# A hybrid decoder layer on one core: another buffer for the bias table, a changed start and a changed end

## The chip, the core and the metric

The kernel runs on one core of one Trainium2 chip. The metric is the device time of one execution in microseconds (us), taken as the median over several runs. Beside the runs there is one execution recorded by the profiler; it has a span (first to last instruction of the program) and a device time of its own. The engines are named as the profile names them: PE is the matrix engine (PEld its weight loads), DVE the vector engine, ACT the scalar engine, POOL GpSimd, SP the engine that here only issues DMA transfers. A "q" behind an engine's name (SPq, ACTq) is its instruction queue, where DMA issues and semaphore instructions appear.

## The reference, cut to what matters

One layer, sequence 256, width 2048, everything in fp32:

```python
n = rmsnorm(h, g_mix);  q, k, v, u = split(n @ w_in)      # 2048 x 5120
a = attention(q, k, v) with a T5 bias: rel_bias[bucket(distance)] is added to the scores
c = silu(layernorm(depthwise_conv31(u_val * sigmoid(u_gate)) + conv_b))
h = h + concat(a, c) @ w_out                              # 2048 x 2048
h = h + cross_attention(rmsnorm(h), rmsnorm(mem))         # 4 heads
h = h + square(relu(rmsnorm(h) @ w1)) @ w2                # 2048 -> 8192 -> 2048
return rmsnorm(h, g_final)
```

With a sequence of 256 and blocks of 256 the block attention is plain causal attention within one block.

## The kernel before, in words

**Weights in 200 steps.** All weights are laid out as 200 pieces of 1 MB (128 x 2048 fp32), one per step. For step j, `raw[j]` is loaded (four buffers, so the load for step j+4 can only start when the split of step j is done with its buffer). ACT rounds it to fp32r into `wh[j]` (lines 157 to 160), DVE subtracts to get the rest `wl[j]`; for one step in seven between 8 and 47 (`on_pool`, line 162: steps 11, 18, 25, ...) POOL makes `wl[j]` in four quarters. Both have three buffers, so `wh[j]` can be written when PE is through with step j-3. PE then runs three products per pair of tiles (high x high, high x low, low x high; `mm3`, from line 101). A step is 48 products with 256 columns or 24 with 512.

**Order of the work.** The order on every engine is written out by hand: the loop over the 200 steps at line 916 issues, for step j, the hooks of the place "early", the load for step j+4, the split of step j+2, the hooks "pre" and "late", and then PE's products with the hooks "mid" and "post" in between and behind. Every engine carries out its own list in that order, so an instruction that waits holds up all behind it. The steps 0 to 15 are the convolution's inputs `u` in four blocks of four, 16 to 23 are v, 24 to 39 q and k, then mem's k and v, `w_out`, the cross attention, and from step 72 the MLP.

**Start.** SP issues all the first loads (lines 127 to 137): the gains, then in turn a quarter of the first group of x (`hT[0]`, line 130) and a quarter of the first weights (`raw[0]`, line 131), then the other groups of x with `raw[1]` to `raw[3]`. For steps 0 to 3 the splits are cut in quarters (line 334 for `wh`, line 186 for the activations `actH`). POOL builds the identity matrix and the ones (lines 139, 140).

**The bias table.** `make_bias` (line 260) takes an 8 x 512 tile from the `ring`, fills it on POOL with one row of bias values per head, and `spread_bias` (line 273, hook "early" of step 8) sends it with one DMA on ACT's queue to DRAM, 128 copies of each row (1024 pieces of 1532 bytes); `load_bias` reads it back in step 20 with each partition shifted by one. The `ring` (line 91) is a tag of seven 128 x 512 buffers, used by nearly all short-lived tiles: the gates of the convolution (`evac_u`, line 389, at steps 7, 8, 12 and 16), the squares of the statistics of mem (`st_m.group` at steps 8 to 11, ACT's line 210, added up by POOL on line 211). `evac_u(i)` also takes one of the four `hp` buffers, into which POOL writes zeros (line 391) and the gated values (line 396), and on which DVE then runs the 31 taps of the convolution as background work.

**End.** The last four steps (196 to 199) are the last column block of `w2`. Steps 196 and 197 do both halves of the rows; step 198 the rows 0 to 127 with the weights of 198 and 199, step 199 the rows 128 to 255 with the same weights. `finish(t, bank)` (line 835) adds the residual, squares with a sum, forms 1/sqrt with one Newton step, scales four 128 x 512 pieces and sends them out; `finish(0)` is issued ahead of the products of step 199, `finish(1)` behind them.

Of the kernel before, what the change touches and what calls it, by code (L numbers as in the profile page):

```python
# [9 lines left out]
F32 = mybir.dt.float32  # L10
# [5 lines left out]
P = 128  # L16
# [23 lines left out]
STEP_US = 5.25  # L40

# [36 lines left out]
def tile_hybrid_block(ctx: ExitStack, tc: tile.TileContext, xT, memT, w, par, rel, gfin, out):  # L78
# [50 lines left out]
    for i in range(4):  # L129
        nc.sync.dma_start(hT[0][:, i, :], xT[:, i, :])  # L130
        nc.sync.dma_start(raw[0][:, i * 512:(i + 1) * 512], w[0, :, i * 512:(i + 1) * 512])
# [6 lines left out]

    make_identity(nc, ident)
    pool.memset(ones, 1.0)  # L140
# [119 lines left out]
    def make_bias():  # L260
        rev = ring((8, 512))
        pool.memset(rev[:, 0:384], MASK)
        d = 0
        while d < T:
            e = d
            while e + 1 < T and bucket(e + 1) == bucket(d):
                e += 1
            b = bucket(d)
            pool.tensor_copy(rev[:, 255 - e:256 - d], relt[:, b:b + 1].to_broadcast([8, e - d + 1]))
            d = e + 1  # L270
        return rev
# [562 lines left out]

    def finish(t, bk):
# [6 lines left out]
        for i in range(2):  # L842
            c = slice(1536 + i * T, 1536 + (i + 1) * T)
            d = acc[t][:, c]
            dve.tensor_tensor(d, bk.ap[:, i * T:(i + 1) * T], d, op=OP.add)
            act.activation(ring()[:, 0:T], d, AF.Square, accum_out=ssq[:, 8 * t + 3 + i:8 * t + 4 + i])
            pool.tensor_mul(d, d, gb[3][:, i * T:(i + 1) * T])
            dve.scalar_tensor_tensor(part_ if i == 0 else v, ssq[:, 8 * t + 3 + i:8 * t + 4 + i], 1.0 / D, part_,
                                     op0=OP.mult, op1=OP.add)
# [3 lines left out]
        dve.tensor_scalar(a, a, -0.5, 1.5, op0=OP.mult, op1=OP.add)  # L853
        dve.tensor_tensor(r, y, a, op=OP.mult)
        for c in (0, 1, 2, 3):
            d = acc[t][:, c * 512:(c + 1) * 512]
            if c in (1, 3):
                act.activation(d, d, AF.Copy, scale=r)
            else:
                dve.tensor_scalar(d, d, r, None, op0=OP.mult)  # L860
            nc.sync.dma_start(out[rows, c * 512:(c + 1) * 512], d)

    for q in range(4):
# [4 lines left out]
        for cb in range(4):  # L868
            jc = j0 + 16 + 4 * cb
            if q == 3 and cb == 3:  # L870
                banks = []

                def first(kg, jc=jc):
# [10 lines left out]
                pe_units[jc + 3] = lambda jc=jc: (  # L884
                    act_stationary(jc + 2, banks, 2, s_pair, False, ts=(1,))
                    + act_stationary(jc + 3, banks, 3, s_pair, True, ts=(1,)))
# [145 lines left out]
```

## Time and profile before

| what | value |
|---|---|
| median of 3 runs | 1175.96 us (1175.51 to 1176.62) |
| the profiled execution, device time | 1174.24 us |
| its span | 1172.4 us |
| instructions | 18441 |
| DVE busy | 707.8 us (60%) |
| ACT busy | 540.9 us (46%) |
| POOL busy | 116.6 us (10%) |
| HBM read, written | 216.18 MB, 3.67 MB |

The profiled execution is 1.84 us longer than its span and 1.72 us shorter than the median of the runs. PE's clock is granted in two levels, full (2.4 GHz, shown as 1.00 or a 9 in the strip of slices) and half (1.2 GHz, 0.50). Matrix products overlap, so what counts is the distance between their starts and not their length. A wait is shown with the instruction that ended it.

### The profile page before, as it was taken

What the parts mean: (1) busy time and instruction counts of PE and PEld (TensorE: products, weight loads), DVE (VectorE), ACT (ScalarE), POOL (GpSimd) and SP (SyncE); (2) the same over time, 40 slices, a digit from 0 to 9 for tenths busy, and PEclk for the clock granted to TensorE, in tenths of its full rate; (3) what the DMA queues carried; (4) which work ended last, traced back from release to release, by engine and by line L of the source; (5) the groups of instructions that cost most, each with busy time, mean ns of one, the idle gap of its engine ahead of it and who ended that gap; (6) DMA issues with size and microseconds to landing.
All of it is one profiled execution on the core that took longest, in us unless ns stands there. A gap on an engine that the chain in (4) does not pass through costs nothing.

```text
span 1172.4 us, 18441 instructions
## 1 busy us (share of the span) xinstructions
PE 1149.8 (98%) x7976; PEld 1073.0 (92%) x7976; DVE 707.8 (60%) x821; ACT 540.9 (46%) x564; POOL 116.6 (10%) x100
## 2 busy tenths in 40 slices
PE   7989999999999999999999999999999999999996
PEld 7988899999999999999889999889999888999885
DVE  6669998787666668555444545454555454445443
ACT  7525444565666456554333444333444333444342
POOL 2453121012003003000000000000000000000112
PEclk9998999999999999999999999999999999999998
DMA  8865654444554535545655544655554655554632
GB/s 340 288 186 180 221 204 169 162 147 177 184 193 168 199 120 180 216 145 192 240 195 200 180 180 175 221 182 199 193 181 150 227 198 182 190 195 153 217 142 72
DMA packets 35000, 221.02 MB, mean 189 GB/s; under 512 B 3816, under 2 KB 6504, under 8 KB 9448
## 3 DMA queue, kind: packets, MB, share of 16 engines
q1 hardware_dynamic: 33888, 218.29, 52.0%
q10 hardware_dynamic: 1032, 1.57, 0.9%
q8 instruction: 62, 1.02, 0.3%
q14 instruction: 18, 0.15, 0.0%
HBM read 216.18 MB, written 3.67 MB: 188 GB/s over the span
## 4 chain that ended last, share of the span: by engine, by line
PE 93%; DMA 4%; ACT 1%; DVE 1%; issue 0%; SPq 0%; ACTq 0%
PE mm L101 87%; PE cv L101 3%; DMA dram_rev<-ring 3%; PE sm L101 2%; DMA raw<-in_w_dram 1%; DVE wl L67 1%; ACT wh L160 0%; PE sm L813 0%; PE sm L499 0%; PE sm L689 0%; DVE small L67 0%; ACT actH L186 0%; ACT L679 0%; ACT ring L679 0%; ACT ring L210 0%
## 5 line engine op out<-in xcount | busy, mean ns | idle before, releaser
L67 DVE TENSOR_TENSOR wl<-raw,wh 128x2048 fp32r<-128x2048 f32 (+1 forms) x205 | 447.1, 2187 | 305.5 <-ACT wh L160 301.1
L160 ACT ACTIVATE wh<-raw 128x2048 fp32r<-128x2048 f32 x195 | 373.5, 1915 | 505.0 <-PE mm L101 462.5
L101 PE MATMUL mm<-actH,wh 128*128 128x256 f32 x1600 | 452.4, 283 | 11.0 <-ACT wh L334 6.3
L101 PE MATMUL mm<-actH,wl 128*128 128x256 f32 x1600 | 449.0, 281 | 1.8 <-DVE wl L67 1.8
L101 PE MATMUL mm<-actL,wh 128*128 128x256 f32 x1600 | 448.4, 280 | 0.0
L101 PEld LDWEIGHTS mm<-actH,wh 128*128 128x128 f32 x1600 | 302.9, 189 | 11.7 <-ACT wh L334 6.5
L101 PEld LDWEIGHTS mm<-actH,wl 128*128 128x128 f32 x1600 | 303.1, 189 | 2.5 <-DVE wl L67 2.5
L101 PEld LDWEIGHTS mm<-actL,wh 128*128 128x128 f32 x1600 | 302.4, 189 | 0.3
L101 PE MATMUL mm<-wh,sH 128*128 128x512 f32 x512 | 199.3, 389 | 0.0
L101 PE MATMUL mm<-wh,sL 128*128 128x512 f32 x512 | 199.2, 389 | 0.0
L101 PE MATMUL mm<-wl,sH 128*128 128x512 f32 x512 | 199.2, 389 | 0.0
L101 PEld LDWEIGHTS mm<-wh,sL 128*128 128x128 f32 x512 | 96.1, 188 | 20.2
L101 PEld LDWEIGHTS mm<-wl,sH 128*128 128x128 f32 x512 | 96.1, 188 | 19.8
L101 PEld LDWEIGHTS mm<-wh,sH 128*128 128x128 f32 x512 | 96.1, 188 | 19.7
L67 DVE SCALAR_TENSOR_TENSOR cv<-hp,part,cv 128x256 f32<-128x256 f32 x240 | 97.7, 478 | 0.0
L897 POOL TENSOR_TENSOR acc<-acc,gb 128x512 f32<-128x512 f32 x6 | 12.1, 2041 | 669.8 <-ACT ring L833 669.8
L67 DVE TENSOR_TENSOR sL<-ring,sH 128x512 fp32r<-128x512 f32 x32 | 22.2, 692 | 67.1 <-ACT sH L801 67.1
L211 POOL TENSOR_TENSOR acc<-acc,ring 128x512 f32<-128x512 f32 x17 | 35.7, 2098 | 163.4 <-ACT ring L210 162.7
L170 POOL TENSOR_TENSOR wl<-raw,wh 128x512 fp32r<-128x512 f32 x24 | 32.4, 1383 | 98.0 <-ACT wh L160 98.0
L101 PE MATMUL mm<-wh,actH 128*128 128x512 f32 x96 | 38.2, 398 | 0.0
L101 PE MATMUL mm<-wh,actL 128*128 128x512 f32 x96 | 37.9, 395 | 0.0
L101 PE MATMUL mm<-wl,actH 128*128 128x512 f32 x96 | 37.9, 395 | 0.0
(156 smaller groups left out, 1039.1 us busy)
## 6 DMA issues: line engine op xcount, KB each, us to landing
raw<-in_w_dram SPq DMA_DIRECT2D x199, 1024.0 KB, 4.8
mem<-in_memT_dram SPq DMA_DIRECT2D x4, 512.0 KB, 8.0
out_dram<-acc SPq DMA_DIRECT2D x8, 256.0 KB, 3.1
hT<-in_xT_dram SPq DMA_DIRECT2D x3, 512.0 KB, 8.2
dram_rev<-ring ACTq DMA_DIRECT2D x1, 1532.0 KB
raw<-in_w_dram SPq DMA_DIRECT2D x4, 256.0 KB, 4.4
bias<-dram_rev SPq DMA_DIRECT2D x1, 1024.0 KB, 9.1
gb<-in_gfin_dram SPq DMA_DIRECT2D x4, 256.0 KB, 7.0
```

Source lines behind the costliest of these rows:

```text
L67: return op(out, *args, **kw)
L101: pe.matmul(o, lhsT=lhsT, rhs=rhs, start=not bk.begun, stop=stop, skip_group_check=True)
L160: act.activation(wh[j], raw[j], AF.Copy)
L170: pool.tensor_sub(wl[j][:, s], raw[j][:, s], wh[j].bitcast(F32)[:, s])
L211: eng.tensor_tensor(self.acc, self.acc, sq, op=OP.add)
L897: pool.tensor_mul(d, d, gb[cb])
```

## The change

- The tile of `make_bias` is taken from the four `hp` buffers, which the convolution's inputs use, and no longer from the `ring`.
- At the start the four quarters of `hT[0]` are issued from ACT's queue; the ones are written ahead of the identity; ACT runs a copy of one column, ahead of which its table is loaded, and PE transposes the ones 14 times into a bank that nobody reads.
- At the end step 199 does its columns in two halves, 256 columns each (48 products in place of 24). `finish` issues both adds, then both squares, then both small sums; the gains are multiplied by -0.5 beforehand on POOL (step 96), which saves one small operation; and the result goes out in five pieces, three scaled by DVE and sent by SP, two scaled and sent by ACT.

```diff
--- before.py
+++ after.py
@@ -38,6 +38,7 @@
 AHEAD = 2
 WOUT_ORDER = [(0, 0), (1, 0), (2, 0), (0, 1), (1, 1), (2, 1), (3, 0), (3, 1)]
 STEP_US = 5.25
+WARM = 14
 
 ROOM = 128
 ACT_SHIFT = {"H0": 16, "H1": 16, "H2": 112, "H3": 112, "L0": 16, "L1": 16, "L2": 112, "L3": 112}
@@ -127,7 +128,7 @@
     nc.sync.dma_start(part[:, 0:CB], par[:, 0:CB])
     load(0)
     for i in range(4):
-        nc.sync.dma_start(hT[0][:, i, :], xT[:, i, :])
+        act.dma_start(hT[0][:, i, :], xT[:, i, :])
         nc.sync.dma_start(raw[0][:, i * 512:(i + 1) * 512], w[0, :, i * 512:(i + 1) * 512])
     for g in range(1, 4):
         nc.sync.dma_start(hT[g], xT[:, 4 * g:4 * g + 4, :])
@@ -136,8 +137,13 @@
     relt = sb.tile([8, N_BUCKETS], F32, name="relt")
     nc.sync.dma_start(relt, rel)
 
+    pool.memset(ones, 1.0)
     make_identity(nc, ident)
-    pool.memset(ones, 1.0)
+
+    act.activation(rr[:, 14:15], ones[:, 0:1], AF.Copy)
+    warm = bank("sm")
+    for i in range(WARM):
+        pe.transpose(warm.ap[:, (i % 4) * P:(i % 4 + 1) * P], ones, ident)
 
 
     hooks = {}
@@ -258,7 +264,9 @@
     bias = sb.tile([P, 8, T], F32, tag="acc0", name="bias")
 
     def make_bias():
-        rev = ring((8, 512))
+
+        rev = sb.tile([P, 2, T + CONV_K - 1], F32, tag="hp", name="rev", bufs=4)
+        rev = rev.rearrange("p a b -> p (a b)")[0:8, 0:512]
         pool.memset(rev[:, 0:384], MASK)
         d = 0
         while d < T:
@@ -832,6 +840,12 @@
         d = acc[t][:, cb * 512:(cb + 1) * 512]
         act.activation(ring(), d, AF.Square, accum_out=ssq[:, 8 * t + cb:8 * t + cb + 1])
 
+    def prepare_gain():
+
+        for g in gb:
+            pool.tensor_scalar(g, g, -0.5, None, op0=OP.mult)
+    at("late", MLP0 + 24, prepare_gain)
+
     def finish(t, bk):
         st = small()
         part_, v, y, a = (st[:, i:i + 1] for i in range(4))
@@ -839,26 +853,42 @@
         rows = slice(t * P, (t + 1) * P)
         dve.tensor_reduce(v, ssq[:, 8 * t:8 * t + 3], axis=AX.X, op=OP.add)
         dve.tensor_scalar(part_, v, 1.0 / D, EPS, op0=OP.mult, op1=OP.add)
-        for i in range(2):
-            c = slice(1536 + i * T, 1536 + (i + 1) * T)
-            d = acc[t][:, c]
+        ends = [acc[t][:, 1536 + i * T:1536 + (i + 1) * T] for i in range(2)]
+        for i, d in enumerate(ends):
             dve.tensor_tensor(d, bk.ap[:, i * T:(i + 1) * T], d, op=OP.add)
+        for i, d in enumerate(ends):
             act.activation(ring()[:, 0:T], d, AF.Square, accum_out=ssq[:, 8 * t + 3 + i:8 * t + 4 + i])
             pool.tensor_mul(d, d, gb[3][:, i * T:(i + 1) * T])
+        for i in range(2):
             dve.scalar_tensor_tensor(part_ if i == 0 else v, ssq[:, 8 * t + 3 + i:8 * t + 4 + i], 1.0 / D, part_,
                                      op0=OP.mult, op1=OP.add)
         act.activation(y, v, AF.Sqrt)
         dve.reciprocal(y, y)
         dve.scalar_tensor_tensor(a, v, y, y, op0=OP.mult, op1=OP.mult)
-        dve.tensor_scalar(a, a, -0.5, 1.5, op0=OP.mult, op1=OP.add)
-        dve.tensor_tensor(r, y, a, op=OP.mult)
-        for c in (0, 1, 2, 3):
-            d = acc[t][:, c * 512:(c + 1) * 512]
-            if c in (1, 3):
+        dve.scalar_tensor_tensor(r, a, -3.0, y, op0=OP.add, op1=OP.mult)
+        for lo, hi, on_act in ((0, 256, False), (1280, 1664, True), (256, 768, False), (1664, 2048, True),
+                               (768, 1280, False)):
+            d = acc[t][:, lo:hi]
+            if on_act:
                 act.activation(d, d, AF.Copy, scale=r)
+                act.dma_start(out[rows, lo:hi], d)
             else:
                 dve.tensor_scalar(d, d, r, None, op0=OP.mult)
-            nc.sync.dma_start(out[rows, c * 512:(c + 1) * 512], d)
+                nc.sync.dma_start(out[rows, lo:hi], d)
+
+    def last_units(jc, banks):
+        units = []
+        for half in range(2):
+            o = banks[1].ap[:, half * T:(half + 1) * T]
+            for kg in (2, 3):
+                def unit(half=half, kg=kg, o=o):
+                    for i in range(4):
+                        hi, lo = s_pair(kg * 4 + i)
+                        c = slice(i * 512 + half * T, i * 512 + (half + 1) * T)
+                        mm3(banks[1], o, (hi[:, P:], lo[:, P:]), (wh[jc + kg][:, c], wl[jc + kg][:, c]),
+                            kg == 3 and i == 3)
+                units.append(unit)
+        return units
 
     for q in range(4):
         j0 = MLP0 + 32 * q
@@ -881,9 +911,7 @@
                 pe_units[jc + 2] = lambda jc=jc: (
                     act_stationary(jc + 2, banks, 2, s_pair, False, ts=(0,))
                     + act_stationary(jc + 3, banks, 3, s_pair, True, ts=(0,)))
-                pe_units[jc + 3] = lambda jc=jc: (
-                    act_stationary(jc + 2, banks, 2, s_pair, False, ts=(1,))
-                    + act_stationary(jc + 3, banks, 3, s_pair, True, ts=(1,)))
+                pe_units[jc + 3] = lambda jc=jc: last_units(jc, banks)
                 at("pre", jc + 3, lambda: finish(0, banks[0]))
                 at("post", jc + 3, lambda: finish(1, banks[1]))
                 continue
```

## Rows read from the trace of the kernel before

**Rows 1.** The page: engines, and the costliest groups (busy, mean ns | idle before).

```profile
PE 1149.8 (98%) x7976; PEld 1073.0 (92%) x7976; DVE 707.8 (60%) x821; ACT 540.9 (46%) x564; POOL 116.6 (10%) x100
...
L67 DVE TENSOR_TENSOR wl<-raw,wh 128x2048 fp32r<-128x2048 f32 (+1 forms) x205 | 447.1, 2187 | 305.5 <-ACT wh L160 301.1
L160 ACT ACTIVATE wh<-raw 128x2048 fp32r<-128x2048 f32 x195 | 373.5, 1915 | 505.0 <-PE mm L101 462.5
...
L897 POOL TENSOR_TENSOR acc<-acc,gb 128x512 f32<-128x512 f32 x6 | 12.1, 2041 | 669.8 <-ACT ring L833 669.8
```

**Rows 2.** The chain that ended last: start us, us, what.

```profile
50.25 36.14 DMA dram_rev<-ring
```

**Rows 3.** Timeline of ACT: start, duration (us), instruction [idle before <- what ended it].

```profile
86.41 0.63 ACT L210 ACTIVATE ring<-mem 128x512 f32<-128x512 f32 x1 [16.77 <-DMA dram_rev<-ring]
```

**Rows 4.** Timeline of PE around the gap.

```profile
83.84 0.28 PE L101 MATMUL mm<-actL,wh 128*128 128x256 f32 x1
83.96 0.28 PE L101 MATMUL mm<-actH,wl 128*128 128x256 f32 x1
88.89 0.58 PE L101 MATMUL mm<-actH,wh 128*128 128x256 f32 x1 [4.65 <-ACT wh L160]
...
91.21 0.58 PE L101 MATMUL mm<-actH,wl 128*128 128x256 f32 x1 [1.53 <-DVE wl L67]
...
97.34 0.28 PE L101 MATMUL mm<-actH,wh 128*128 128x256 f32 x1
```

**Rows 5.** A stretch: length, busy (count) PE PEld DVE ACT POOL, clock, DMA, GB/s.

```profile
91.00:97.00 6.00, 5.79 (x27) 5.79 (x28) 6.00 (x10) 3.31 (x4) 5.92 (x5) 0.50 0.50 176
```

**Rows 6.** The load of step 13: timeline of SP; DMA issues, us to landing.

```profile
58.14 0.33 SPq L125 DMA_DIRECT2D raw<-in_w_dram  x1
...
raw<-in_w_dram SPq DMA_DIRECT2D x1, 1024.0 KB, 18.7
```

**Rows 7.** Timeline of POOL, 55 to 73 us.

```profile
55.34 0.15 POOL L391 MEMSET hp<- 128x60 f32 x1
...
67.48 5.06 POOL L170 TENSOR_TENSOR wl<-raw,wh 128x512 fp32r<-128x512 f32 x4
```

**Rows 8.** Three stretches at the start, columns as in group 5.

```profile
3.00:4.00 1.00, 0.00 (x0) 0.00 (x0) 0.00 (x0) 0.60 (x1) 0.00 (x0) 1.00 0.64 172
...
6.00:10.00 4.00, 3.70 (x16) 3.48 (x17) 3.26 (x6) 2.81 (x6) 0.00 (x0) 1.00 0.97 318
10.00:14.00 4.00, 4.00 (x28) 4.00 (x28) 1.18 (x2) 1.14 (x2) 0.00 (x0) 1.00 1.01 419
```

**Rows 9.** Timeline of the first 16 us.

```profile
3.40 1.28 ACT L186 ACT_TABLE_LOAD   x1 [3.40 <-DMA hT<-in_xT_dram]
...
14.28 0.63 ACT L334 ACTIVATE wh<-raw 128x512 fp32r<-128x512 f32 x1 [1.95 <-DMA raw<-in_w_dram]
...
15.69 0.39 PE L101 MATMUL mm<-actH,wl 128*128 128x256 f32 x1 [0.22 <-DVE wl L67]
```

**Rows 10.** The end of the chain that ended last.

```profile
1162.85 0.43 DVE acc L67
...
1163.31 0.52 ACT ring L846 x2
...
1164.38 0.52 ACT ring L846 x2
...
1165.80 0.16 DVE small L67
...
1166.18 0.72 ACT acc L858
```

**Rows 11.** Timeline of the last products (PE) and last issues (SP).

```profile
1162.20 0.39 PE L101 MATMUL mm<-wl,sH 128*128 128x512 f32 x1
1162.42 0.39 PE L101 MATMUL mm<-wh,sL 128*128 128x512 f32 x1
...
1166.69 1.81 SPq L861 DMA_DIRECT2D out_dram<-acc  x4
```

## The prediction, made before the changed kernel was run

> **What bounds the kernel now.** I read the page first. PE is busy for 98% of the span while DVE is at 60% and ACT at 46% [rows 1], and ACT's main idle time before a split ended on PE: the weights are made ready in time and PE sets the pace. So time can only be won where PE is not at its pace, and I looked for such places along the chain that ended last. It runs through PE nearly everywhere, with three exceptions: the first 15.7 us, the last ten, and one piece of 36.14 us in between that is a single transfer, the bias rows on their way to DRAM [rows 2].
>
> **The gap.** The timeline of ACT says why that transfer is on the chain. The transfer reads a tile of the ring, and ACT's seventh new ring tile behind it (two gates of step 8, then the squares of mem: one in step 8, two in step 9, the second of two in step 10) gets the same buffer. ACT stands for 16.77 us until the transfer is done [rows 3]. Behind it in ACT's list is the split of step 13. PE, which has two steps of weights in hand, runs dry at 84.08, gets two products at 88.89 and is only under way again at 91.21, at half its clock [rows 4, 5]. The loss can be counted. Products start 0.12 us apart before the gap. The one at 97.34 is the 31st of step 13: two at 88.89, and 28 from 91.21 on, ahead of it. Without the gap the 31st would start at 84.08 + 30 x 0.12 = 87.7. So the gap costs 97.34 - 87.7 = 9.7 us, 2.7 of them because the 29 products from 91.21 on took 6.13 us where 3.5 would do.
>
> **Part 1, the source of the transfer.** It moves to an `hp` buffer, and the ring has no transfer in it any more. What comes next in place of the wait: ACT is free at 69.6 and takes the split of step 13 when its weights are there. They were issued at 58.14 and took 18.7 us [rows 6], so they are there at 76.8; this load does not depend on the gap. With 1.9 us on ACT and 2.2 on DVE [rows 1] the split ends at 81.0, or 82 with the squares of mem in front and POOL at work beside DVE. PE wants it at 84.08. That is 2 us to spare, the tightest place of my forecast, but to spare.
> The new wait is in `evac_u`. With four `hp` buffers given out in turn (the table, then u blocks 0, 1, 2) the block at step 16 gets the table's buffer back, and its zeros on POOL wait for the transfer, which ends at 50.25 + 36.14 = 86.4, perhaps some us later with more weights moving beside it. POOL has nothing behind these zeros but the gates of step 16 and the quarter splits of step 18; step 16 starts at 84.08 + 3 x 5.65 = 101 at PE's pace (48 products a step). About 14 us of cover. I put this part at 9.7 us; between 9.0 (small waits left) and 9.7.
>
> **Part 2, the start.** PE's pace begins at 15.69, and that is set by the landing of `raw[1]`: ACT begins its split at 14.28, after idling for it [rows 9]. The table load of 1.28 us in front of the first split, and the quarters of x, are not on that path by themselves. PE's first step is at half clock (16 products from 6.3 to 10 us) [rows 8]; it has 48 products and would end hardly before 14.6, so faster transfers alone would also win little. The change does both.
> DMA first: in the fourth us the engines were at a share of 0.64, and the us before and behind look alike; from 6 us on they are full [rows 8]. If a second queue fills these three us, the stream ends about 3 x 0.36 = 1.1 us earlier; if not, 0. A DMA issue takes 1.81 / 4 = 0.45 us on its queue [rows 11], and SP is rid of four. ACT has them now: 1.8 us from about 0.7, then the table load, so it is ready at about 4.2, ahead of the 4.7 of before. The idle share speaks for issuing as the limit, so I take 0.7, nearer to that row.
> The Trainium skill's page "Trainium Kernel Development and Optimization", section "Key Constraints", speaks against the second queue: transfers issued from several engines share the same 16 DMA engines, and only the issuing time is saved. By it alone the start would win 0 wherever the engines are full, and the sum below would be 10.5 in place of 11.2.
> The 14 transposes: no row has one at half clock. As bounds take 0 and the 0.23 us of a product with 256 columns at half clock (3.70 us by 16) [rows 8]: at most 14 x 0.23 = 3.2 us, from about 1.6 us, when POOL has the identity ready, to 4.8. PE had no work until 6.3, so they are free. They should let step 0 run at full clock, which is needed for the 0.7 but adds nothing to it.
>
> **Part 3, the end.** Step 199 has 48 products of 256 columns for 24 of 512. The long ones start 0.22 to 0.23 apart [rows 11], the short ones half of 0.24 [rows 4]: about 0.25 us more, on the path. What it could win is the first half's add and square beside the second half's products. I take that as not happening: no row shows DVE reading one half of a bank while PE writes the other; in the nearest row the add begins 0.43 us after the start of the bank's last product [rows 10, 11]. Bounds: nothing, or the 0.52 us of one square.
> The Trainium skill's page "PSUM — Partial Sum Buffer", section "PSUM bank collisions raise a hardware error", says that two engines in one bank and the same partitions collide even on different columns, so reads are to be held back by bank. By that rule the adds wait for all 48 products, as I have it.
> Even so the chain is shorter. The second square starts at once behind the first, at 1163.85 in place of 1164.38 [rows 10]: 0.53 us. One small operation of 0.16 plus its gap of 0.03 goes [rows 10]: 0.19. Together 0.72, less 0.25: 0.47.
> Output: the last issue of before ends 1166.69 + 1.81 - 1166.18 = 2.3 us after the scaling starts [rows 10, 11]. After, ACT scales 384 columns in about 0.57 (three quarters of its 0.72 plus a fixed part), issues in 0.45, and again: 2.0. So 0.3; between -0.2 (the megabyte itself is the limit) and 0.7. Sum of the end: 0.8, between 0 and 1.7.
> The four products of the gains on POOL in step 96 cost up to 2.0 us each [rows 1]; POOL idles for hundreds of us there, and DVE, which shares its time badly with POOL, is at 60%. They cost nothing; without that cover a few tenths.
>
> **Sum.** 9.7 + 0.7 + 0.8 = 11.2 us. The profiled execution had 1174.24; it would have 1163.0. The median of the runs is 1.72 above it, so 1175.96 - 11.2 = 1164.8 is what I predict.
>
> **The rivals.**
> *The front wins nothing* (the shared engines, part 2): 1175.96 - 10.5 = 1165.5. For: the share is 1.01 from 10 us on; against: 0.64 in the fourth. 10%.
> *The adds run beside the products*: 0.5 more, 1164.3. 6%.
> *The clock falls at the start*: step 0 done early, PE waits for `raw[1]`, and step 1 starts at half clock. The gap shows the price, 2.7 us: 1167.5. In the trace PE lost its clock over an idle time of 4.7 us [rows 4, 5]; here I expect 2 or less. 6%.
> *Step 13 late*: if its weights land 2 to 5 us later than 76.8, PE idles and may lose its clock: up to 1171. 5%.
> *The wait stays on the ring*, because its next tile in turn is also held by something slow: only parts 2 and 3 remain, 1174.5. Nothing in the trace shows such a holder. 2%.
> *Slower*: the block of step 8, not that of step 16, gets the table's `hp` buffer. Its zeros, done at 55.34 in the trace, then wait until 86.4 on POOL, and behind them are gates, three sums of squares and the quarters of step 11 [rows 7]. These began 12.1 us behind the zeros, so at 98.5; the first quarter is there at 99.8, and PE wanted it at 72.8. That is 27 us and 2.7 for the clock, less the 11.2: about 1194. It decides if a freed buffer is taken before those never used; the ring speaks against it, since there the freed buffer came round only as the seventh [rows 3]. 2%.
> The forecast itself keeps 69%.
>
> **The numbers.** Own range of the forecast 1163.2 to 1166.4. With both ends of the start and the end, the clock case and half a microsecond of spread between runs: 1162.5 to 1168.0. What is left out is the late split, the two cases of the wait and a part of the rest. 0.2% is 2.35 us, about what a measurement of this kernel can tell from no change; 0.96 for faster by more than that, 0.02 within, 0.02 slower.
>
> **What would show it.** In the profile of after: no wait of ACT for `dram_rev`; products 0.12 us apart through 84 to 97 us and a clock of 1.00 in that slice; DVE's split of step 13 ending 2 us ahead of PE; POOL's zeros of the fourth block behind the transfer, with PE undisturbed. At the start PE's pace from about 15.0. At the end both adds back to back behind the last product, the scaling about 2.6 us behind it, last issues from two queues. I would be wrong in the main term if PE still had a gap between 80 and 100 us, and in a small one if the first add of the last rows began before the last product.

## The result, and the profile after

In the first series of runs the changed kernel took 1163.05 us (median of 4 runs, 1162.63 to 1164.51), the kernel before 1176.29 (4 runs): a ratio of 0.9888, 95% interval 0.9871 to 0.9905, so 13.2 us less. In the last series it was 1162.9 (4 runs) against 1174.44 (9 runs): 0.9896 (0.9883 to 0.991), 11.5 us less. The prediction was 11.2 us less.

The first rows of the page of the changed kernel, to hold against [rows 1]:

```profile
span 1162.7 us, 18533 instructions
...
PE 1148.5 (99%) x8014; PEld 1072.3 (92%) x8014; DVE 709.2 (61%) x821; ACT 540.3 (46%) x565; POOL 123.0 (11%) x104
```

The span is 9.8 us shorter; DVE, ACT and PE have the same work. The helper lines have moved by a few (L101 is now L102, L160 is L166).

**The gap.** The list of waits from 60 to 105 us (who waited for what: us in total, times, longest):

```profile
ACT wh L166 <- DMA raw<-in_w_dram: 8.0, 1, 8.0
...
POOL hp L399 <- DMA dram_rev<-rev: 1.2, 1, 1.2
PEld sm L102 <- DVE acc L68: 1.1, 1, 1.1
```

ACT's wait for the bias transfer [rows 3] is not there. In its place ACT waits 8.0 us for the weights of step 13, which costs PE nothing at step 13 itself, and POOL 1.2 us for the transfer before it clears the buffer of the fourth block, long before that block's step. The load of step 13, as in [rows 6]:

```profile
57.40 0.33 SPq L126 DMA_DIRECT2D raw<-in_w_dram  x1
...
raw<-in_w_dram SPq DMA_DIRECT2D x1, 1024.0 KB, 20.0
```

It landed at 57.40 + 20.0 = 77.4. The timeline of PE, where [rows 4] had the gap:

```profile
83.21 0.28 PE L102 MATMUL mm<-actH,wl 128*128 128x256 f32 x1
83.33 0.28 PE L102 MATMUL mm<-actH,wh 128*128 128x256 f32 x1
83.44 0.28 PE L102 MATMUL mm<-actL,wh 128*128 128x256 f32 x1
...
91.69 0.28 PE L102 MATMUL mm<-actH,wl 128*128 128x256 f32 x1
92.88 0.61 PE L102 MATMUL sm<-ones,acc 128*128 128x1 f32 x4 [0.92 <-DVE acc L68]
93.35 0.36 PE L102 MATMUL mm<-actH,wh 128*128 128x256 f32 x1
```

The product at 83.33 is the first of step 13, with 0.12 us to its neighbours on either side: no gap. The five us in which PE stood are now full, at full clock (stretch, with the columns of [rows 5]):

```profile
84.00:89.00 5.00, 5.00 (x45) 5.00 (x44) 5.00 (x8) 1.99 (x2) 3.81 (x5) 1.00 0.65 229
91.00:97.00 6.00, 5.08 (x44) 4.88 (x43) 6.00 (x9) 1.31 (x2) 0.00 (x0) 1.00 0.54 194
```

But between 91.69 and 92.88, within step 14, PE stands for one small product, the column sums of mem's statistics, which needs a sum from DVE. Two rows of DVE's timeline say why:

```profile
90.22 2.28 DVE L68 TENSOR_TENSOR wl<-raw,wh 128x2048 fp32r<-128x2048 f32 x1
92.42 0.41 DVE L68 TENSOR_TENSOR acc<-acc 128x256 f32<-128x256 f32 x1
```

The sum (0.41 us, from 92.42) is queued behind the split of step 15, and that split behind all that the late weights of step 13 have pushed back. The profiles below bear this out: PE stands here where that load took 19.9 us or more, and not where it took 18.9 or less.

**The start.** The same instructions as in [rows 9], and the transposes:

```profile
1.49 3.25 PE L146 MATMUL sm<-ident,ones 128*128 128x128 f32 x14 [1.49 <-POOL ident masks.py:199]
2.62 1.28 ACT L143 ACT_TABLE_LOAD   x1 [2.62 <-issue]
...
13.53 0.63 ACT L342 ACTIVATE wh<-raw 128x512 fp32r<-128x512 f32 x1 [1.95 <-DMA raw<-in_w_dram]
...
14.94 0.38 PE L102 MATMUL mm<-actH,wl 128*128 128x256 f32 x1 [0.22 <-DVE wl L68]
```

```profile
3.00:4.00 1.00, 1.00 (x7) 1.00 (x6) 0.00 (x0) 0.99 (x2) 0.00 (x0) 1.00 0.91 171
...
6.00:10.00 4.00, 2.84 (x17) 2.24 (x18) 2.23 (x5) 2.17 (x5) 0.00 (x0) 1.00 1.04 374
```

The DMA share of the fourth us rose from 0.64 to 0.91 [rows 8]. From 6 to 10 us PE did 17 products in 2.84 us of busy time in this profile, where it had needed 3.70 for 16. Its pace starts at 14.94, 0.75 us earlier.

**The end.** The last product, the end of the chain that ended last, POOL's part, and the last issues, as in [rows 10, 11]:

```profile
1153.98 0.28 PE L102 MATMUL mm<-wh,sL 128*128 128x256 f32 x1
...
1154.30 0.44 DVE acc L68
...
1154.76 0.92 ACT ring L860 x4
...
1155.70 0.40 DVE small L68
...
1156.80 0.17 DVE rr L68
...
1157.06 0.62 ACT acc L873
...
1155.34 1.41 POOL L861 TENSOR_TENSOR acc<-acc,gb 128x256 f32<-128x256 f32 x2 [4.24 <-ACT ring L860]
...
1157.38 1.31 SPq L877 DMA_DIRECT2D out_dram<-acc  x3
...
1158.76 0.34 ACTq L874 DMA_DIRECT2D out_dram<-acc  x1
```

Both adds begin behind the last product (1153.98 + 0.28 = 1154.26). The scaling starts 2.70 us after the first of them on DVE (1157.00; on ACT 1157.06), where it was 3.33 [rows 10]; from there to the end of the span it is 5.68 us in place of 6.26.

The ledger of the two profiled executions, each line a difference of two times in the same rows of both:

| part | before | after | won, us |
|---|---|---|---|
| PE's pace starts | 15.69 | 14.94 | 0.75 |
| from there to the first product of step 14 | 83.78 | 74.04 | 9.74 |
| step 14 | 6.23 | 7.28 | -1.05 |
| first product of step 15 to that of step 199 | 1051.51 | 1052.09 | -0.58 |
| step 199, to the end of its last product | 5.60 | 5.91 | -0.31 |
| last product to the scaling | 3.37 | 2.74 | 0.63 |
| scaling to the end of the span | 6.26 | 5.68 | 0.58 |
| span | 1172.44 | 1162.68 | 9.76 |

In the other profiles with the same end 2.74 repeats within 0.01 us and 5.68 within 0.03, but for one 5.57. The kernel before was profiled once.

### The profile page after: what moved, and what is told of

It is laid out like the page before. It is cut to its first block, busy times and chain, and to the rows that moved or that the text cites. A ratio compares the mean times of both kernels' runs of the same rounds, so it can differ in the third digit from the quotient of the medians.

```text
span 1162.7 us, 18533 instructions
## 1 busy us (share of the span) xinstructions
PE 1148.5 (99%) x8014; PEld 1072.3 (92%) x8014; DVE 709.2 (61%) x821; ACT 540.3 (46%) x565; POOL 123.0 (11%) x104
## 4 chain that ended last, share of the span: by engine, by line
PE 93%; DMA 3%; DVE 2%; ACT 1%; issue 0%; ACTq 0%; POOL 0%; DVEq 0%
PE mm L102 87%; PE cv L102 3%; DMA raw<-in_w_dram 2%; PE sm L102 2%; DVE wl L68 1%; ACT wh L166 0%; DVE cv L68 0%; DMA hT<-in_xT_dram 0%; PE sm L821 0%; PE sm L507 0%; PE sm L697 0%; DVE small L68 0%; ACT actH L192 0%; POOL hp L404 0%; ACT L687 0%
## 5 line engine op out<-in xcount | busy, mean ns | idle before, releaser
L166 ACT ACTIVATE wh<-raw 128x2048 fp32r<-128x2048 f32 x195 | 373.6, 1916 | 512.2 <-PE mm L102 463.7
L102 PE MATMUL mm<-actH,wh 128*128 128x256 f32 x1600 | 449.9, 281 | 2.5 <-ACT wh L342 2.5
L102 PE MATMUL mm<-actH,wl 128*128 128x256 f32 x1600 | 446.4, 279 | 0.7 <-DVE wl L68 0.7
L102 PE MATMUL mm<-actL,wh 128*128 128x256 f32 x1600 | 446.0, 279 | 0.0
L102 PEld LDWEIGHTS mm<-actH,wh 128*128 128x128 f32 x1600 | 300.3, 188 | 3.5 <-ACT wh L342 3.3
L102 PEld LDWEIGHTS mm<-actH,wl 128*128 128x128 f32 x1600 | 300.6, 188 | 1.3 <-DVE wl L68 1.3
L102 PEld LDWEIGHTS mm<-actL,wh 128*128 128x128 f32 x1600 | 299.7, 187 | 0.3
L102 PE MATMUL mm<-wh,sH 128*128 128x512 f32 (+1 forms) x520 | 200.7, 386 | 0.0
L102 PE MATMUL mm<-wh,sL 128*128 128x512 f32 (+1 forms) x520 | 200.6, 386 | 0.0
L102 PE MATMUL mm<-wl,sH 128*128 128x512 f32 (+1 forms) x520 | 200.6, 386 | 0.0
L102 PEld LDWEIGHTS mm<-wh,sH 128*128 128x128 f32 x520 | 97.7, 188 | 19.7
L102 PEld LDWEIGHTS mm<-wh,sL 128*128 128x128 f32 x520 | 97.7, 188 | 19.7
L102 PEld LDWEIGHTS mm<-wl,sH 128*128 128x128 f32 x520 | 97.7, 188 | 19.5
L102 PE MATMUL mm<-wh,actH 128*128 128x512 f32 x96 | 38.2, 398 | 0.0
L102 PE MATMUL mm<-wh,actL 128*128 128x512 f32 x96 | 38.0, 395 | 0.0
L102 PE MATMUL mm<-wl,actH 128*128 128x512 f32 x96 | 38.0, 395 | 0.0
```

What stands on the lines that cost most here:

```text
L102: pe.matmul(o, lhsT=lhsT, rhs=rhs, start=not bk.begun, stop=stop, skip_group_check=True)
L166: act.activation(wh[j], raw[j], AF.Copy)
```

## The experiments

The theory: the gap is worth 9.7 us and is gone, what its transfer does to the load of step 13 gives about 1 us of it back, the start and the end bring a little under 1 us each. The rivals: the start, the end or the clock bring more than that, or the convolution's buffers are held up.

### The table back on the ring

```diff
-        rev = sb.tile([P, 2, T + CONV_K - 1], F32, tag="hp", name="rev", bufs=4)
-        rev = rev.rearrange("p a b -> p (a b)")[0:8, 0:512]
+        rev = ring((8, 512))
```

> The changed kernel with the bias table back on the ring; start and end as changed. Theory (the wait on the ring is worth 9.7 us, less 1.1 given back at the sums of mem): ACT waits 15 us or more for the transfer again, PE has one gap of about 5 us near 83 us and some 29 products at half clock behind it, and the time is 1174 us, about 2 below the kernel before. Rival (start and end bring more than the one profile shows, since the medians lie 13.2 us apart and the two spans only 9.8): 1172.5 or less.

Measured: 1172.59 us (10 runs) against 1175.09 (13 runs), ratio 0.998 (0.997 to 0.9989). Waits from 60 to 105 us, and the two stretches around the gap (columns as in [rows 5]):

```profile
ACT ring L216 <- DMA dram_rev<-ring: 15.6, 1, 15.6
...
DVE wl L68 <- ACT wh L166: 10.3, 1, 10.3
...
82.00:88.00 6.00, 1.85 (x14) 1.44 (x12) 1.18 (x1) 3.64 (x5) 1.81 (x2) 0.99 0.14 52
88.00:95.00 7.00, 5.83 (x28) 5.83 (x29) 7.00 (x10) 4.27 (x4) 6.92 (x5) 0.52 0.41 151
```

The wait, the gap and the half clock (28 products from 88 to 95 us at 0.52) are back, with the start and the end of the changed kernel in place. The gap cost 8.3 us in this profile (82.36 us from the start of PE's pace, 14.81, to the first product of step 14, 97.17, where the changed kernel needs 74.04), 9.7 in the profile of before. The time lies between the two figures expected: 2.5 us below the kernel before, with an interval from 1.3 to 3.5, which holds the theory's 2; the rival's bound of 1172.5 was missed by 0.1 us only. By medians, each against the kernel before in its own series, 9.0 to 10.7 us of the changed kernel's gain (11.5 and 13.2, less 2.5) hang on the buffer alone. The rest is for start and end together, and for the gap, which came out shorter here.

### A buffer of its own for the table

```diff
-        rev = sb.tile([P, 2, T + CONV_K - 1], F32, tag="hp", name="rev", bufs=4)
-        rev = rev.rearrange("p a b -> p (a b)")[0:8, 0:512]
+        rev = sb.tile([8, 512], F32, name="rev")
```

> The changed kernel with a buffer of its own for the bias table, neither the ring's nor the convolution's. Theory (POOL's new wait for the transfer is covered): no wait of POOL for the transfer, and the span within 0.5 us of the changed kernel's. Rival (the convolution's buffers are held up by it): 1 us or more below it.

Measured: span 1160.3 us, one run of 1162.09, and POOL's wait for the transfer gone. That is 2.4 us below the first profile of the changed kernel, but only 1.2 below its second (next experiment), and the first product of step 14 comes 74.03 us after the start of PE's pace, to the hundredth as in the changed kernel. What differs is step 14 (6.10 us against 7.28 and 6.22), and the long stretch behind it. The span missed the theory's 0.5 us and met the rival's figure. But five later versions that leave the table in the convolution's buffer have the same 6.10 in step 14 (the start of before, no transposes, one queue, the bank of its own and the long products), and 1051.1 to 1051.6 us from step 15 to 198 as this one has 1051.12. So the convolution's buffer holds nothing up; the span alone would not have told.

### The changed kernel again

> The changed kernel once more, for a second profile. Theory: PE's pace starts at 14.9 us, no gap at 84 us, a gap of about 1.1 us near 92 us, last product to end about 8.4 us; the spread between runs is in the small gap and in the transfers, so each part repeats within 0.5 us. Rival (one of the parts itself varies by 2 us or more between runs, which would explain why the medians differ by more than the profiles): the start of PE's pace or the gap near 92 us differs by more than 1 us.

Measured: span 1161.5, and in the last series another profile with 1161.25. The three profiles of the same program, with two more:

| profile | pace starts | to step 14 | step 14 | steps 15 to 198 | span |
|---|---|---|---|---|---|
| changed, first | 14.94 | 74.04 | 7.28 | 1052.09 | 1162.7 |
| changed, second | 14.70 | 74.04 | 6.22 | 1052.21 | 1161.5 |
| changed, third | 14.41 | 74.03 | 7.27 | 1051.21 | 1161.2 |
| own buffer | 14.71 | 74.03 | 6.10 | 1051.12 | 1160.3 |
| before | 15.69 | 83.78 | 6.23 | 1051.51 | 1172.4 |

The wait in step 14 was there in two of three profiles. The weights of step 13 landed 20.0, 18.9 and 19.9 us after their issue in the three, and 17.7 to 18.5 us after it in the six versions with 6.10 in step 14 (own buffer and the five named there), so the wait hangs on about one us of this load. The stretch that PE paces alone, steps 15 to 198, differs by 1 us between runs of one program, and the -0.58 of the ledger is such a difference. The theory's "each part within 0.5 us" was too tight by that, and the rival's threshold for step 14 was just passed.

### The sums of mem one step later

```diff
-    at("mid", 14, st_m.totals, 2)
-    at("mid", 14, lambda: st_m.chain(r_m), 2)
+    at("mid", 15, st_m.totals, 2)
+    at("mid", 15, lambda: st_m.chain(r_m), 2)
```

> The changed kernel with the column sums of mem's statistics one step later (step 15). Theory (in the changed kernel PE stands 1.1 us in step 14 for a small DVE sum queued behind the late split of step 15): that gap is gone, span 1.1 us below the changed kernel's. Rival (the delay only moves to the next thing that DVE owes PE): a gap of 0.5 us or more shows up at the split of step 15 or 16, span less than 0.5 us below.

Measured: span 1160.8, step 14 at 5.66 us (48 products and nothing else), step 15 at 6.09 with the sums in it, and no product of PE waits for DVE from 60 to 105 us. But this run did not put the theory to the test: its load of step 13 took 18.5 us, as in the versions without the wait, whose steps 14 and 15 take the same 11.75 us together (6.10 and 5.65). That the edit removes the wait where the load is late is argued from the first profile alone: the sum ends there at 92.8, and the middle of step 15 would come at about 97.4 (an estimate: step 15 from 94.6, and the sums 2.8 us behind its start, as in step 14).

### The start of before

```diff
-        act.dma_start(hT[0][:, i, :], xT[:, i, :])
+        nc.sync.dma_start(hT[0][:, i, :], xT[:, i, :])
...
+    make_identity(nc, ident)
     pool.memset(ones, 1.0)
-    make_identity(nc, ident)
-
-    act.activation(rr[:, 14:15], ones[:, 0:1], AF.Copy)
-    warm = bank("sm")
-    for i in range(WARM):
-        pe.transpose(warm.ap[:, (i % 4) * P:(i % 4 + 1) * P], ones, ident)
```

> The changed kernel with the start of before: all transfers on SP, no transposes of the ones, no early table load. Theory (the start is worth 0.7 to 1.0 us, through the landing of the second weights): the second weights are split from 14.2 us on, PE's pace starts at 15.7 us, and everything behind is about 0.8 us later than in the changed kernel. Rival (the start brings nothing that lasts, as the same 16 DMA engines carry all): PE's pace starts within 0.3 us of the changed kernel's 14.9.

Measured: the second weights split from 13.73, PE's pace from 15.14. Between the two theories: 0.2 later than the changed kernel's first profile and 0.7 later than its third. One profile does not decide it.

### Without the transposes

```diff
-    warm = bank("sm")
-    for i in range(WARM):
-        pe.transpose(warm.ap[:, (i % 4) * P:(i % 4 + 1) * P], ones, ident)
```

> The changed kernel without the 14 transposes. Theory (step 0 then runs at half clock to about 11 us, but waits for its quarters and for the second weights at 13.5 us anyway): PE's pace starts within 0.4 us of the changed kernel's 14.9. Rival (the clock is what the start wins): 0.7 us later or more.

Measured: PE's pace from 14.19, earlier than in any run with the transposes. They win nothing here. Without them the products of step 0 start 0.21 us apart up to 9.7 us and 0.12 later; the first product of step 1 still follows at 13.60, and what sets the pace is the low part of the second weights, for which PE waits 0.19 us even then.

The other profiles say the same. With the transposes, step 0 starts with products 0.12 us apart in four profiles of eleven; in the other seven, the changed kernel's third among them, they are 0.21 apart from the fourth on, as without. The pace does not follow it: with two queues it starts at 14.68 in the mean of the four and in that of the other six alike.

### One queue again, transposes and table load kept

```diff
-        act.dma_start(hT[0][:, i, :], xT[:, i, :])
+        nc.sync.dma_start(hT[0][:, i, :], xT[:, i, :])
```

> The changed kernel with the four quarters of x back on SP's queue, transposes and early table load kept. Theory (the idle share of the DMA engines before 5 us is what the second queue fills): the split of the second weights starts about 14.2 us in place of 13.5, PE's pace 0.7 us later. Rival (shared engines, the second queue brings nothing): both within 0.2 us of the changed kernel.

Measured: PE's pace from 16.18. The split of the second weights in the three runs (one queue; start of before; no transposes), with the fourth us of the first and the last, and the stretch from 6 to 10 us of the first:

```profile
14.78 0.63 ACT L342 ACTIVATE wh<-raw 128x512 fp32r<-128x512 f32 x1 [1.95 <-DMA raw<-in_w_dram]
...
3.00:4.00 1.00, 1.00 (x7) 1.00 (x6) 0.00 (x0) 0.49 (x1) 0.00 (x0) 1.00 0.54 139
6.00:10.00 4.00, 3.92 (x17) 3.70 (x18) 2.70 (x5) 2.60 (x6) 0.00 (x0) 1.00 1.00 291
```

```profile
13.73 0.63 ACT L338 ACTIVATE wh<-raw 128x512 fp32r<-128x512 f32 x1 [2.10 <-DMA raw<-in_w_dram]
```

```profile
12.78 0.63 ACT L339 ACTIVATE wh<-raw 128x512 fp32r<-128x512 f32 x1 [2.10 <-DMA raw<-in_w_dram]
...
3.00:4.00 1.00, 0.00 (x0) 0.00 (x0) 0.00 (x0) 0.99 (x2) 0.00 (x0) 1.00 0.63 163
```

The share of the fourth us is 0.54 with one queue and 0.91 in the changed kernel, but it does not sort the runs: without the transposes it is 0.63 with two queues, and the kernel before had 0.64 with one. What sorts them is what had been moved by 10 us: 2.07 to 2.09 MB in the three profiles with one queue, 2.41 to 2.55 MB in the eleven with two. Most of that difference arises from 6 to 10 us, where the share is near 1 either way (291 to 318 GB/s with one queue, 358 and more with two). All profiles of the study together: with one queue PE's pace starts at 15.14, 15.69 and 16.18 (mean 15.67), with two queues at 14.19 to 15.04 in eleven profiles (mean 14.64). The groups don't overlap, though the nearest two are 0.1 us apart. By the means the second queue is worth 1.0 us; single runs scatter by half a us around it. The early table load was not tried by itself.

### The last half columns in a bank of their own

```diff
+        if t == 1:
+            dve.tensor_tensor(ends[1], tail[0].ap[:, T:2 * T], ends[1], op=OP.add)
...
+        tail.append(bank("mm"))
...
-            o = banks[1].ap[:, half * T:(half + 1) * T]
+            bk = (banks[1], tail[0])[half]
+            o = bk.ap[:, half * T:(half + 1) * T]
...
-                        mm3(banks[1], o, (hi[:, P:], lo[:, P:]), (wh[jc + kg][:, c], wl[jc + kg][:, c]),
+                        mm3(bk, o, (hi[:, P:], lo[:, P:]), (wh[jc + kg][:, c], wl[jc + kg][:, c]),
```

> The changed kernel with the last 24 products (the second half of the columns of step 199) in a bank of their own; the first bank's sums are added while they run, and one add more is made for the second half behind them. Theory (in the changed kernel both adds wait for all 48 products because they share one bank): the first add starts about 2.8 us before the last product ends, one add and one square leave the chain, the scaling starts about 2.1 us behind the last product in place of 2.75, span 0.6 us below. Rival (the bank is not what holds the add back): the first add starts behind the last product here too, and nothing is won.

Measured: span 1159.9. The timeline of its last us:

```profile
1150.53 0.74 DVE L68 TENSOR_TENSOR acc<-mm,acc 128x256 f32<-128x256 f32 x2
...
1151.29 0.42 ACT L862 ACTIVATE ring<-acc 128x256 f32<-128x256 f32 x1 [0.42 <-DVE acc L68]
...
1151.78 0.28 PE L102 MATMUL mm<-wh,sL 128*128 128x256 f32 x1
...
1152.10 0.42 DVE L68 TENSOR_TENSOR acc<-mm,acc 128x256 f32<-128x256 f32 x1 [0.82 <-PE mm L102]
...
1154.18 0.35 DVE L68 TENSOR_SCALAR acc<-acc,rr 128x256 f32<-128x256 f32 x1
```

The first two adds start at 1150.53, while PE writes the other bank, and the first square is done before the last product ends (1152.06). They come later than expected, 1.5 us ahead of that end and not 2.8: PE was through with the first bank at 1149.2, but DVE was still scaling the first rows' result. The scaling starts 2.08 us after the last add began, against 2.70: 0.62 us won. With one bank the change's halves did not bring this.

### Long products in step 199

```diff
-                pe_units[jc + 3] = lambda jc=jc: last_units(jc, banks)
+                pe_units[jc + 3] = lambda jc=jc: (
+                    act_stationary(jc + 2, banks, 2, s_pair, False, ts=(1,))
+                    + act_stationary(jc + 3, banks, 3, s_pair, True, ts=(1,)))
```

> The changed kernel with the products of step 199 as before, 24 with 512 columns in place of 48 with 256, everything else as changed. Theory (the halves win nothing in one bank and cost PE 0.3 us): step 199 takes 5.6 us in place of 5.9, the first add still begins behind the last product, the scaling 2.7 us behind it, span 0.3 us below the changed kernel's but for its start. Rival (the halves do win something): the scaling starts later than 2.8 us behind the last product.

Measured: span 1160.1; the first add starts behind the last product and the scaling 2.70 us behind that add, to the hundredth as with the halves. The halves win nothing in one bank; in the changed kernel they cost PE 0.31 us (5.91 against the 5.60 of before).

### The transfer cut into eight

```diff
-    def spread_bias():
-        act.dma_start(dram_rev.rearrange("h (p j) -> h p j", p=P),
-                      rev[:, 0:383].unsqueeze(1).to_broadcast([8, P, 383]))
+    def spread_bias(h):
+        act.dma_start(dram_rev[h:h + 1, :].rearrange("h (p j) -> h p j", p=P),
+                      rev[h:h + 1, 0:383].unsqueeze(1).to_broadcast([1, P, 383]))
...
-    at("early", 8, spread_bias)
+    for h in range(8):
+        at("early", 7 + h, lambda h=h: spread_bias(h))
```

> The changed kernel with the table's transfer cut into eight, one head per step from step 7 to 14, in place of one transfer of 1024 pieces at step 8. Theory (the one transfer keeps the load of step 13 from landing for 18 us or more, which leaves DVE late and PE now and then waiting for the sums of mem in step 14): every load between 55 and 95 us lands within 13 us of its issue, ACT's wait of 8 us for the weights of step 13 is gone, and PE has no wait at step 14. Rival (the loads are late because of the bytes, not of the one queue entry): the longest landing is still above 15 us.

Measured: 1166.8 us, span 1165.0, in one run, 2.3 us above the slowest of nine runs of the changed kernel. The loads issued between 60 and 75 us landed only after 18 to 22 us. Waits from 60 to 110 us; a stretch of step 14; and the page's row of the queue that carries the table (packets, MB, share of all 16 engines over the span), first here, then in the changed kernel and in the kernel before:

```profile
ACT wh L166 <- DMA raw<-in_w_dram: 19.3, 5, 9.4
POOL hp L399 <- DMA dram_rev<-rev: 16.1, 1, 16.1
...
PEld sm L102 <- DVE acc L68: 3.2, 1, 3.2
...
92.00:99.00 7.00, 4.38 (x27) 4.39 (x28) 7.00 (x9) 3.19 (x2) 0.00 (x0) 0.81 1.00 209
...
q10 hardware_dynamic: 2304, 2.88, 3.4%
```

```profile
q10 hardware_dynamic: 2184, 2.88, 1.2%
```

```profile
q10 hardware_dynamic: 1032, 1.57, 0.9%
```

ACT waits 19.3 us for weights, PE 3 us for the same small sum in step 14, and the clock falls (0.81 in this stretch); step 14 takes 10.7 us. In the kernel before the queue carries the table alone, 0.9%; the changed kernel's row adds quarters of x and pieces of the result, which are the same in both versions here. So the table's share rose by 2.2%, from 0.9% to about 3.1%: a piece of 1532 bytes took about 0.56 us of an engine's time in place of 0.16, by these shares. The remedy failed, and the rival's sign came (landings above 15 us). Whether the single transfer holds up the load of step 13 in the changed kernel stays open, as the pieces themselves became dearer here. The number of transfers, the partitions that each reads and perhaps the engines that carry it changed together; which of them makes a piece dear was not tried further.

### Both remedies together

The two edits of "the sums of mem one step later" and "the last half columns in a bank of their own".

> The changed kernel with the sums of mem one step later and the last half columns in a bank of their own. Theory: 0.6 us from the end in every run, and up to 1.1 us in those runs in which the load of step 13 lands late; 1.0 us below the changed kernel's median in the same call, whose time is about 1163. Rival (the spread between runs swallows both): within 0.4 us of it.

> The changed kernel itself in the same call. Theory (9.7 us from the gap, 0.9 from the start, 0.9 from the end, 0.5 lost where PE's products lie a little further apart behind step 30): 11.0 to 12.0 us below the kernel before. Rival (the 13.2 us of the first medians): 12.7 or more.

Measured: 1162.14 us for the two edits (5 runs; 0.9888 of the kernel before, 0.9873 to 0.9902), 1162.9 for the changed kernel (4 runs; 0.9896, 0.9883 to 0.991). The medians differ by 0.8 us, about what was expected, but the intervals overlap: the spread between runs is as large. In the profiles the part at the end shows: the scaling starts 2.08 us after the last add's start, against 2.70. Steps 14 and 15 took 11.75 us together against 12.93, but the load of step 13 took 18.7 us in this profile and 19.9 in the changed kernel's, so here too the worth of the later sums is not shown. For the changed kernel the 11.5 us lie in the theory's range.

## Why the prediction was right

**The gap.** Predicted 9.7, found 9.74 up to step 14, in every profile of the changed kernel within 0.01. The count of products gave it. The reason holds too: with the ring's buffer back, the wait, the gap and the half clock came back. ACT's next wait was named rightly (the weights of step 13, at 76.8 predicted, 77.4 found), and so was POOL's wait for the transfer, which is covered: the table in a buffer of its own changed nothing up to step 14. The rival in which the block of step 8 gets the table's buffer falls with that, and so does the one in which the ring still waits.

**What I missed.** "2 us to spare, the tightest place" was followed only as far as the split of step 13, which ended as I said ("81.0, or 82", found 81.7). DVE's list goes on, and behind the split of step 15 a sum of 0.41 us for mem's statistics, which PE takes as a product in the middle of step 14, comes late by 1.05 us in two of three profiles. The step of my text that failed is the one from a split in time to no loss: I didn't ask what else is queued behind it that PE waits for without a buffer in between. With it part 1 brought 8.7 us in that profile (9.74 - 1.05), just below the range I gave it (9.0 to 9.7).

**The start.** Predicted 0.7, found 0.75 in the first profile and 1.0 over all profiles, and by the runs through the second queue, not the transposes; I had set the transposes at nothing by themselves and said they were needed for the 0.7. They are not: without them the pace started at 14.19, with step 0 through at 13.6 and not "hardly before 14.6". The rival of the shared engines, by the Trainium skill's page "Trainium Kernel Development and Optimization", section "Key Constraints", falls in this case: with one queue alone changed back, the pace started at 16.18, later than in any profile with two. Its exception, the issuing time, fits: the quarters of x are issued from 0.72 to 2.13 us in place of 1.18 to 4.01. But the row I took the 0.7 from, the idle share of the fourth us, does not tell the two kinds of run apart, and most of the bytes are won between 6 and 10 us, where I had called the engines full. Why engines that are equally busy move more there stays open, so the size came out for a reason that is only half shown. ACT's "about 4.2" was a slip: its own terms add up to 3.8, and ACT was ready at 3.90. The clock did not fall in the changed kernel's three profiles; it did in the version with a buffer of its own (below), at no cost to PE's pace, which started at 14.71.

**The end.** Predicted 0.8, found 0.90. PE's extra 0.31 (0.25 said), the chain 0.63 (0.72), the output 0.58 (0.3). The second square brought 0.67 and not 0.53, as it starts 0.41 us behind the first, and the saved operation 0.19 as said, but the small sum took 0.23 back, see below. The output was under-sized: I took the end of the last issue as the measure (2.0 us after the scaling starts, found 1158.76 + 0.34 - 1157.00 = 2.1, against 2.3 before), and the stretch from there to the end of the span is 0.35 us shorter too. Whether smaller last pieces or the second queue shortened it was not tried. The halves did not overlap, as the bank rule of the Trainium skill's page "PSUM — Partial Sum Buffer", section "PSUM bank collisions raise a hardware error", had it. In the trace this is a wait of DVE for PE's last product; in the run with two banks the first add waits no longer, so the shared bank was the obstacle. What the chip does with an add beside the products of its own bank was not tried.

**The sum.** 11.2 predicted; 9.8 in the first pair of profiles, 11.2 with the third profile, 13.2 and 11.5 by medians. The first median, 1163.05, lies 0.15 us below the forecast's own range (1163.2 to 1166.4) and inside the wide one. I had added the 1.72 us by which the median of before lay above its profiled execution; in the changed kernel the profiled execution, 1164.51 for the 1163.0 I said, was the slowest of its four runs and lay 1.46 above the median. So the parts came out 1.4 us short in that profile, and the median 1.75 us under the forecast, which no part accounts for: that the number landed so near has luck in it. The kernel before ran at 1176.29, 1175.09 and 1174.44 in three series, and its own profiled execution, 1174.24, was below all four runs of the first. What varies in the kernel before was not profiled a second time. The gap differs between the two profiles with the table on the ring (9.7 us in the kernel before, 8.3 in the changed kernel with the ring back); that this explains the difference between the medians is not shown.

## What to carry to other kernels

A buffer that a slow transfer reads should not rotate with the buffers of short-lived tiles: the wait comes many allocations later, on an engine that has nothing to do with the transfer. When such a wait is removed, follow the late engine's list until the first thing that a pacing engine takes directly, not only to the next split. Splitting work by columns to overlap the evacuation needs a bank per half; in one bank it only adds products.

## What the runs showed of the hardware that was not expected

A small DVE operation on one element per partition, the second small sum, took 0.38 us in place of 0.16. The first and the second in DVE's timeline:

```profile
1155.30 0.16 DVE L68 SCALAR_TENSOR_TENSOR small<-ssq,small 128x1 f32<-128x1 f32 x1 [0.24 <-ACT ring L860]
1155.70 0.38 DVE L68 SCALAR_TENSOR_TENSOR small<-ssq,small 128x1 f32<-128x1 f32 x1 [0.24 <-ACT ring L860]
```

The second ended at 1156.08, just when POOL's product of the first half (1155.34, the first of the two in its row) was through, at 1156.07. Before, that product ran while DVE had nothing small to do. The Trainium skill's page "SBUF — State Buffer", section "Who interferes with whom", says that a DVE instruction with two SBUF inputs contends with a POOL instruction that reads SBUF, over a shared pair of ports that is "an exclusive lock"; the rows agree, here and in the other profiles with the end as changed (0.38 to 0.39 us in four of them). In the version with two banks the sum took 0.16 again, with POOL's first product out of its way.

The slow first products are not shown as a lower clock. In the kernel before and in the one without transposes the products of step 0 start 0.21 us apart, in the first two profiles of the changed kernel 0.12 and in its third 0.21 again, and the granted clock of the stretch from 6 to 10 us is 1.00 in all of them. In the version with a buffer of its own the products of step 0 began 0.12 apart, and from 8.0 to 11.2 us they were 0.21 apart at a granted clock of 0.50. The changed kernel's third profile, then that version:

```profile
6.00:10.00 4.00, 3.88 (x17) 3.66 (x18) 2.81 (x6) 2.85 (x7) 0.00 (x0) 1.00 1.05 397
```

```profile
8.20:11.20 3.00, 3.00 (x16) 3.00 (x15) 2.57 (x6) 2.15 (x5) 0.00 (x0) 0.50 1.05 396
```

My text called step 0 "at half clock"; its distance is that of the half clock, but its rows say 1.00, and which of the two is right no run settles.

And eight transfers of 192 KB, whose 128 pieces each read the same partition, took three to four times the engine time of one transfer of the same bytes from eight partitions (about 3.1% against 0.9% by the page's shares). The weights loaded beside them landed 18 to 22 us after their issue; what makes the pieces dear was not settled.
